# Weight parts kept by the second token group, retention chunks cut at the token blocks, and five early product pairs in an FFN

## The chip, the cores and the metric

The kernel runs on one core of one Trainium2 chip. TensorE (PE) multiplies matrices into PSUM, which has 8 banks; VectorE (DVE), ScalarE (ACT) and GpSimd (POOL) work beside it; SyncE (SP) issues most of the DMAs. The metric is the device time of one execution in microseconds. The time before is 2477.27 us, the median of 3 runs (2476.28 to 2477.57).

## What is computed

One layer of a hybrid decoder for 2048 prompt tokens and 8 sample tokens (one new token for each of 8 sequences), all in float32. Cut to what matters:

```python
h = rmsnorm(x, g_mix) * (1 + scale_m) + shift_m
q, k, v, g_ret, x_lru, g_lru = split(h @ w_in)          # 1024 -> 4*512 + 2*512
o, s_ret = retention(rotary(q), rotary(k), v, s_ret)     # 4 heads of 128, chunkwise
ret_out = silu(g_ret) * groupnorm(o)
hl = rg_lru(causal_dwconv(x_lru))                        # 512 channels, a scan over time
lru_out = hl * gelu(g_lru)
x = x + gate_m * (concat(ret_out, lru_out) @ w_out)
h = rmsnorm(x, g_ffn) * (1 + scale_f) + shift_f
f = (gelu(causal_dwconv(h @ w_up_conv)) * (h @ w_up_gate)) @ w_down   # 1024 -> 2816 -> 1024
x = x + gate_f * f
y = rmsnorm(x, g_final)
```

The six shifts, scales and gates come from the conditioning vector c by one more matrix, w_ada. The retention, LRU and convolution states are outputs too. Retention may be cut into chunks of any width: a chunk's scores are taken within it, and the state carries the rest.

## The kernel before

**Precision.** Each float32 operand is split into a high part that TensorE's reduced float32 holds and a low part, the rest; each product is three matmuls (`mm3`, L356: high by high, high by low, low by high, lines 358 to 360). Splitting a 128x512 piece of a weight (`parts`, L283) is a copy on ACT (L288) and a subtraction (L289) on the engine `lo_on`, POOL or DVE. The two parts, 128x1024, are written to a DRAM tile named by their key (L295), and whoever fetches the key later loads both parts from there (L286) and splits nothing. A w_in tile of 128 columns has two halves, each a key with `(h,)` added; w_out and w_down keys are one 128x512 piece; FFN keys are one left operand of a product (below). The first eight parts written in the first group are parked in `unsaved` and stored between items 4 and 7 (L1382).

**Groups and blocks.** The tokens go through the layer in three groups (`GROUPS`, L38): 688, 680 and 680 prompt tokens, the third with the 8 sample tokens behind them. A group has two blocks of 344 (340 in the second). Activations lie with channels on the partitions, so a matmul streams one block, 344 columns.

**Items.** `group_items` (L1180) writes each group's work as a list of items: weight keys, a rate, and a function. The main loop (L1379) fetches keys ahead of the items (`LOOK` is 4, a w_in or w_ada key counts 2), runs the function, and then advances two lists of generators: `soon` (normalisations, LRU chains) by the rate's whole part, and `bg` (the retention of a head) by the rate as a credit, 1 where it is 2. The order in one group: head 0, LRU 0, head 1, out-projection of head 0 (16 items), LRU 1, head 2, out of head 1 (16 items at rate 0.5), LRU 2 and 3, head 3 (its items by block: Q, K, V, gate of block 0, then of block 1), out of heads 2 and 3 (16 items of 12 matmuls, block 0 first), then the FFN. An out item of heads 2 and 3 waits until the retention of head 3 has ended its block.

The list sets priorities and the order of dependences; the framework's planner then fixes each engine's own order when the kernel is built, by its model of durations. Each engine runs its list in order. A tile comes from a pool with a fixed number of buffers, and whoever asks for one more waits for a release: the pool `f` has 12 (FFN operands and mixer outputs), `t` 10 (block-sized scratch), PSUM `pm` 3 (projections, down products, some early FFN products) and `pt` 5.

**Retention** (`ret`, L617) runs through chunks of 128 tokens with a shorter last one (six in a group). Step i does part a of chunk i (transposes, scores), part b of chunk i-1 (output and state) and part c of chunk i-2 (normalised and gated output). When the last chunk that touches a block is through part c, the block is split for the out-projection (L686). In the third group the sample tokens' steps (`ret_samples`, L692) are run at step `at`: 0, or 3 for head 3. The rate of head 3's block-1 items is 0.5 (L1196).

**FFN.** The 22 tiles of 128 channels are taken in 11 pairs, and each pair, for each of the two up-projections, with the two blocks and the two halves of the 1024 inputs, is a 2x2 block product with seven products in place of eight (`PRODUCTS`, L51): P1 and P2 need only block 0 (b11, b21); P5 needs t1, P6 t2, P3 b22, P7 t3 and P4 t4, which are made on DVE and ACT from both blocks (`operands2`, L925). P1 is added into several results: for an ordinary pair by going on in its PSUM bank, for an `apart` pair by DVE from a copy (`keep`, L997). In each group four pairs of products P1 and P2 come early, those of pairs 0 and 1 of both kinds, before the operands of block 1 are there; pair 1 is `apart`, with P1 and P2 in two banks of `pm`. P2's result goes through `up_out` (copy, convolution, GeLU) or `gate_out` (multiply, split into f tiles). Behind pair i come the 16 down items of pair i-1, between its products.

In the first group the 14 left operands of pair 0 are prepared ahead (`ahead`, L1272): split, stored and dropped, one behind each item of rate 0.5 or more from the out-projection of head 1 on.

Of the kernel before, what the change touches and what calls it, by code (L numbers as in the profile page):

```python
# [57 lines left out]
WIDTHS = sorted({w for _, n, _, _ in GROUPS for w in ((P,) if n % P == 0 else (P, n % P))}, reverse=True)  # L58
# [32 lines left out]
def hybrid_step(ctx: ExitStack, tc: tile.TileContext, I, O):  # L91
# [169 lines left out]
    unsaved = []  # L261
# [20 lines left out]

    def parts(key, w, src=None, lo_on=G):  # L283

        if src is None:
            nc.sync.dma_start(out=w.bitcast(F32), in_=split[key])  # L286
        else:
            S.activation(out=w[:, 0:512], in_=src, func=AF.Copy)  # L288
            lo_on.tensor_tensor(out=w[:, 512:1024], in0=src, in1=w[:, 0:512].bitcast(F32), op=ALU.subtract)  # L289
            nm = "_".join(str(v) for v in key)  # L290
            split[key] = dp.tile([P, 1024], F32, tag=nm, name=nm)
            if len(unsaved) < 2 * FIRST:
                unsaved.append((split[key], w))
            else:
                nc.sync.dma_start(out=split[key], in_=w.bitcast(F32))  # L295
        return [w[:, 512 * i:512 * i + 512].rearrange("p (k c) -> p k c", c=P) for i in range(2)]
# [29 lines left out]
    def fetch_operand(key, lo_on):  # L326
# [25 lines left out]
        if i == 1 and nm in ("A11", "A12"):  # L352
# [106 lines left out]
    class Group:  # L459
        def __init__(g, gi):  # L460
# [4 lines left out]
            g.chunks = [(c, min(P, g.ntok - c)) for c in range(0, g.ntok, P)]  # L465
# [151 lines left out]
        def ret(g, p):  # L617
# [46 lines left out]
            at = 0 if p < H - 1 else LAG + 1  # L664
            for i in range(nch + LAG):
# [16 lines left out]
                if 0 <= i - LAG:  # L682
                    part_c(*g.chunks[i - LAG], pst("oT") if q is None else q[:, 384:512])
                    for b in g.blocks:
                        if i == nch + LAG - 1 if b[1] == g.TC else sum(g.chunks[i - LAG]) >= b[1] > g.chunks[i - LAG][0]:
# [311 lines left out]
        def keep(g, q, name, more=None):  # L997
            t = ttile(name)
# [7 lines left out]
        def quad_item(g, st, kind, i, what, out, apart):  # L1006

            left, right, bank, start = PRODUCTS[what]
            early = what in ("P1", "P2") and i < 2
            q = g.product(st, (kind, i, left), right, bank, start or apart and what == "P6",  # L1010
                          psm if early and (apart or what == "P2") else pst)
            p1 = st.get("p1")
            if what == "P1":
                st["p1"] = g.keep(q, "p1")
# [4 lines left out]
            elif what == "P2":  # L1019
                out(2 * i, 0, q, p1, apart)  # L1020
                if not apart:
                    del st["p1"]
# [7 lines left out]
        def up_out(g, ft, l, q, more, stays=False):  # L1030
# [49 lines left out]
        def gate_out(g, ft, l, q, more, stays=False):  # L1080
            n = g.n
            cv = g.cv.pop((ft, l))[:, 0:n]
            if more is not None:
                t = (ttile("gv") if stays else more)[:, 0:n]
# [95 lines left out]
    def group_items(g, nxt):  # L1180
# [6 lines left out]
        def head(p, by_block=False):  # L1187
# [5 lines left out]
            for n, (j, b) in enumerate(jb):  # L1193
                if n == 4 and early:
                    add([], 0, lambda: (drain(bg), bg.append(g.ret(p))))
                add([("w_in", 512 * j + P * p)] if b == g.blocks[0] else [], 0.5 if n >= 4 and early else 1,  # L1196
# [37 lines left out]
        def quad(kind, i, what, rate=1):  # L1234
            st = quads.setdefault((kind, i), {})
            out_fn = g.up_out if kind == "w_up_conv" else g.gate_out
            add([(kind, i, PRODUCTS[what][0])], rate, g.quad_item, st, kind, i, what, out_fn, i == 1)
# [18 lines left out]
        UP, GATE = "w_up_conv", "w_up_gate"  # L1256
        seq = ("P1", "P5", "P6", "P2", "P7", "P3", "P4")
# [3 lines left out]
        out.extend(out_((0,), both, 0.25))  # L1261
        lru(1)
        head(2)
        n = len(out)
# [25 lines left out]
        for i in range(1, np_):  # L1290
# [3 lines left out]
            some = [(kind, what) for kind in (UP, GATE) for what in seq if i > 1 or what not in ("P1", "P2")]  # L1294
# [84 lines left out]
    for n, (keys, rate, fn, a) in enumerate(items):  # L1379
        if FIRST <= n < 2 * FIRST:  # L1380
            for dst, w in unsaved[2 * (n - FIRST):2 * (n - FIRST) + 2]:
                nc.sync.dma_start(out=dst, in_=w.bitcast(F32))  # L1382
        if n == 3:
# [50 lines left out]
```

## Time and profile before

| | us |
|---|---|
| median of 3 runs | 2477.27 |
| the profiled execution | 2479.54 |
| its span, first to last instruction | 2477.8 |
| TensorE busy in it | 2376.3 |
| mean granted TensorE clock | 0.984 of full |

The span is what the profile covers; the execution's own time is 1.7 us longer. A granted clock under 1.00 in a stretch means that TensorE ran part of it at half speed. The stretches that matter in each group are these (us from the start of the span):

| | first group | second | third |
|---|---|---|---|
| first projection of head 0 | 29.8 | 899.1 | 1669.0 |
| out-projection of head 1 | 229.9 | 1059.1 | 1837.6 |
| head 3 | 320.5 | 1117.2 | 1899.3 |
| out-projection of heads 2 and 3 | 353.9 | 1148.8 | 1933.6 |
| first FFN product | 401.0 | 1191.5 | 1986.3 |
| last down product | 899.3 | 1669.1 | 2466.1 |

### The profile page before, as it was taken

How to read it: one execution, taken by the hardware profiler on the slowest of the kernel's cores; microseconds unless marked ns; L12 is line 12 of the kernel's file. 1: busy time of each engine (PE TensorE's matmuls, PEld its weight loads, DVE VectorE, ACT ScalarE, POOL GpSimd, SP SyncE). 2: the span in 40 equal slices, each digit the busy share in tenths (PEclk: the TensorE clock that was granted, in tenths of full speed). 3: DMA queues.
4: the chain of work that ended last, by engine and by line, in shares of the span. 5: the costliest groups of instructions: out<-in, count | busy, mean ns of one | idle time of the engine just before them, and what ended most of it. 6: DMA issues, size and time to landing. Idle time of an engine off the chain costs nothing.

```text
span 2477.8 us, 40044 instructions
## 1 busy us (share of the span) xinstructions
PE 2376.3 (96%) x15157; PEld 2279.8 (92%) x15157; DVE 1433.9 (58%) x3159; ACT 857.4 (35%) x1935; POOL 701.5 (28%) x729
## 2 busy tenths in 40 slices
PE   6999888999999999999899999999999889999998
PEld 4988688999999899999899999999998889999998
DVE  4645567866676665665753434346666575454444
ACT  4323453544444534232422222243125242222222
POOL 3443440466666723222001010112123100101011
PEclk8999889999999999999999999999999999999999
DMA  9576875788878865333666676765332455667674
GB/s 347 179 259 212 298 249 191 265 291 297 303 285 308 313 226 180 116 110 120 210 216 244 215 246 214 252 215 193 131 121 89 147 209 200 243 214 245 213 249 165
DMA packets 233220, 543.89 MB, mean 220 GB/s; under 512 B 19191, under 2 KB 100711, under 8 KB 233020
## 3 DMA queue, kind: packets, MB, share of 16 engines
q1 hardware_dynamic: 231948, 539.87, 62.6%
q8 instruction: 120, 1.97, 0.3%
q10 hardware_dynamic: 696, 0.91, 0.1%
q0 software_dynamic: 384, 0.56, 0.1%
q14 instruction: 72, 0.59, 0.1%
HBM read 392.96 MB, written 148.42 MB: 218 GB/s over the span
## 4 chain that ended last, share of the span: by engine, by line
PE 57%; DVE 5%; issue 1%; ACT 1%; DMA 1%; POOL 1%; POOLq 0%; SPq 0%; DVEq 0%; ACTq 0%
PE down L359 6%; PE down L358 6%; PE down L360 6%; PE qx L359 4%; PE qx L360 4%; PE qx L358 4%; PE proj L358 4%; PE proj L360 4%; PE proj L359 4%; PE qz L358 2%; PE qz L359 2%; PE qz L360 2%; PE qy L359 1%; PE qy L360 1%; PE qy L358 1%
## 5 line engine op out<-in xcount | busy, mean ns | idle before, releaser
L836 DVE SCALAR_TENSOR_TENSOR x<-down,mod,x 128x344 f32<-128x344 f32 (+2 forms) x624 | 348.2, 568 | 351.4 <-PE down L360 346.8
L358 PE MATMUL proj<-hh,wb 128*128 128x344 f32 (+1 forms) x1152 | 380.5, 330 | 10.5 <-DVE rotb L609 4.3
L359 PE MATMUL proj<-hl,wb 128*128 128x344 f32 (+1 forms) x1152 | 373.7, 324 | 0.0
L360 PE MATMUL proj<-hh,wb 128*128 128x344 f32 (+1 forms) x1152 | 373.7, 325 | 0.0
L359 PE MATMUL qx<-op,wb 128*128 128x344 f32 (+1 forms) x1056 | 337.6, 320 | 5.9 <-DVE op L906 5.8
L443 POOL TENSOR_TENSOR ffl<-cv,ffh 128x344 fp32r<-128x344 f32 (+1 forms) x120 | 123.6, 1036 | 764.0 <-ACT ffh L442 696.9
L358 PE MATMUL qx<-op,wb 128*128 128x344 f32 (+1 forms) x1056 | 336.9, 320 | 2.7 <-ACT op L905 1.4
L360 PE MATMUL qx<-op,wb 128*128 128x344 f32 (+1 forms) x1056 | 336.5, 319 | 0.0
L358 PE MATMUL down<-ffh,wb 128*128 128x344 f32 (+1 forms) x960 | 305.0, 324 | 5.1 <-DVE x L836 5.0
L360 PE MATMUL down<-ffh,wb 128*128 128x344 f32 (+1 forms) x960 | 306.2, 320 | 0.3 <-POOL wb L289 0.3
L359 PE MATMUL down<-ffl,wb 128*128 128x344 f32 (+1 forms) x960 | 306.1, 319 | 0.0
L289 POOL TENSOR_TENSOR wb<-wr,wb 128x512 fp32r<-128x512 f32 x146 | 203.5, 1402 | 167.3 <-ACT wb L288 138.3
L358 PEld LDWEIGHTS proj<-hh,wb 128*128 128x128 f32 x1152 | 219.3, 190 | 25.1 <-issue 11.2
L359 PEld LDWEIGHTS proj<-hl,wb 128*128 128x128 f32 x1152 | 219.9, 191 | 2.6 <-issue 0.6
L360 PEld LDWEIGHTS proj<-hh,wb 128*128 128x128 f32 x1152 | 219.3, 190 | 2.5 <-issue 0.9
L359 PEld LDWEIGHTS qx<-op,wb 128*128 128x128 f32 x1056 | 198.6, 188 | 7.6 <-DVE op L906 7.6
L358 PEld LDWEIGHTS qx<-op,wb 128*128 128x128 f32 x1056 | 198.6, 188 | 3.9 <-ACT op L905 2.0
L1061 DVE SCALAR_TENSOR_TENSOR cv<-u,vec,cv 128x344 f32<-128x344 f32 (+2 forms) x264 | 171.4, 667 | 48.5 <-ACT cv L1041 46.5
L360 PEld LDWEIGHTS qx<-op,wb 128*128 128x128 f32 x1056 | 198.4, 188 | 0.0
L358 PEld LDWEIGHTS down<-ffh,wb 128*128 128x128 f32 x960 | 179.3, 188 | 11.1 <-DVE x L836 10.2
L360 PEld LDWEIGHTS down<-ffh,wb 128*128 128x128 f32 x960 | 180.4, 188 | 0.8 <-POOL wb L289 0.8
L359 PEld LDWEIGHTS down<-ffl,wb 128*128 128x128 f32 x960 | 180.6, 188 | 0.0
(313 smaller groups left out, 4856.4 us busy)
## 6 DMA issues: line engine op xcount, KB each, us to landing
wb<-w_down SPq DMA_DIRECT2D x100, 512.0 KB
wb<-w_in SPq DMA_DIRECT2D x96, 512.0 KB
wb<-w_up_conv_S SPq DMA_DIRECT2D x92, 512.0 KB
wb<-w_up_gate_S SPq DMA_DIRECT2D x92, 512.0 KB
wb<-w_up_conv_A SPq DMA_DIRECT2D x69, 512.0 KB
wb<-w_up_gate_A SPq DMA_DIRECT2D x69, 512.0 KB
w_in<-wb SPq DMA_DIRECT2D x48, 512.0 KB
w_up_conv_S<-wb SPq DMA_DIRECT2D x44, 512.0 KB
```

What stands on the lines that cost most here:

```text
L289: lo_on.tensor_tensor(out=w[:, 512:1024], in0=src, in1=w[:, 0:512].bitcast(F32), op=ALU.subtract)
L358: T.matmul(out, wh, xh, start=first, stop=False, skip_group_check=more)
L359: T.matmul(out, wh, xl, start=False, stop=False, skip_group_check=more)
L360: T.matmul(out, wl, xh, start=False, stop=last, skip_group_check=more)
L443: G.tensor_tensor(out=lo[:, 0:n], in0=src, in1=hi[:, 0:n].bitcast(F32), op=ALU.subtract)
L836: V.scalar_tensor_tensor(out=xs, in0=q[:, 0:np_], scalar=modv[:, jg, m, 0:1], in1=xs, op0=ALU.mult, op1=ALU.add)
L1061: V.scalar_tensor_tensor(out=cv[:, 0:np_], in0=u[:, j:j + np_], scalar=cfw[:, j, ft:ft + 1], in1=cv[:, 0:np_], op0=ALU.mult, op1=ALU.add)
```

## The change

- **Weight parts.** `unsaved` is gone. For the keys that `late` names (w_in tiles of heads 0 and 3 and of LRU 2 and 3, so 24 of the 48 halves, and w_out rows of heads 2 and 3, 8 of 16 pieces) the first fetch splits and stores nothing; the second group fetches the raw piece again, splits it again and stores it; the third loads the parts.
- **Chunks** end with the blocks: 128, 128, 88 twice in the first group (128, 128, 84 in the second; 88 and 80 in the third), six as before. The samples' steps of head 3 run at step 5, and head 3's block-1 items have rate 1.
- **Early pairs.** Five: pairs 0 and 1 of both kinds and pair 2 of `w_up_conv`. The last three are `apart`, and their P1 and P2 now go into one bank of `pm`: P1 is copied, and P2 is added on top in PSUM. P1 of the three come first, then P2 of the three. Pair 1's P1 copies lie in f tiles.
- **Ahead.** The 14 operands of pair 0 are spread: 0.45 of one per full item, from LRU 1 on.
- The raw A11 and A12 of pair 2 of `w_up_conv` are loaded twice, the low parts of pair 2's weights are made on DVE in the first group, and the small transposes and LRU constants come at item 6 in place of 3.

```diff
+def chunks_of(gi):
+    _, n, _, edges = GROUPS[gi]
+    ends = [min(e, n) for e in edges]
+    return [(c, min(P, e - c)) for s, e in zip(ends, ends[1:]) for c in range(s, e, P)]
...
-    unsaved = []
+    once = set()
...
+    def late(key):
+        kind, a = key[0], key[1]
+        if kind == "w_in":
+            t = a // P
+            return t % 4 == 3 or t >= 16 and t % 4 == 2 or t < 16 and t % 4 == 0
+        return kind == "w_out" and a % 512 >= 2 * P
...
+            if late(key) and key not in once:
+                once.add(key)
+                return [w[:, 512 * i:512 * i + 512].rearrange("p (k c) -> p k c", c=P) for i in range(2)]
             split[key] = dp.tile([P, 1024], F32, tag=nm, name=nm)
-            if len(unsaved) < 2 * FIRST:
-                unsaved.append((split[key], w))
-            else:
-                nc.sync.dma_start(out=split[key], in_=w.bitcast(F32))
+            nc.sync.dma_start(out=split[key], in_=w.bitcast(F32))
...
-        if i == 1 and nm in ("A11", "A12"):
+        if (i == 1 or i == 2 and kind == "w_up_conv") and nm in ("A11", "A12"):
             del pr[nm]
...
-            at = 0 if p < H - 1 else LAG + 1
+            at = 0 if p < H - 1 else nch - 1
...
-                        if i == nch + LAG - 1 if b[1] == g.TC else sum(g.chunks[i - LAG]) >= b[1] > g.chunks[i - LAG][0]:
+                        if sum(g.chunks[i - LAG]) == b[0] + g.npr(b):
...
             left, right, bank, start = PRODUCTS[what]
-            early = what in ("P1", "P2") and i < 2
-            q = g.product(st, (kind, i, left), right, bank, start or apart and what == "P6",
-                          psm if early and (apart or what == "P2") else pst)
+            if apart:
+                bank = "y" if what in ("P1", "P2") else bank
+                start = what in ("P1", "P5", "P6")
+            q = g.product(st, (kind, i, left), right, bank, start,
+                          psm if bank == "y" and i < 3 else pst)
             p1 = st.get("p1")
             if what == "P1":
-                st["p1"] = g.keep(q, "p1")
+                st["p1"] = g.keep(q, "p1", pool=fp if i == 1 else None)
...
-                out(2 * i, 0, q, p1, apart)
-                if not apart:
-                    del st["p1"]
+                out(2 * i, 0, q, None if apart else st.pop("p1"))
...
-                add([("w_in", 512 * j + P * p)] if b == g.blocks[0] else [], 0.5 if n >= 4 and early else 1,
+                add([("w_in", 512 * j + P * p)] if b == g.blocks[0] else [], 1,
...
+        early = ((UP, 1), (GATE, 1), (UP, 2))
...
         out.extend(out_((0,), both, 0.25))
+        n = len(out)
         lru(1)
         head(2)
-        n = len(out)
...
+        due = 0.0
         for it in its:
             out.append(it)
-            if ahead and it[1] >= 0.5:
+            due += 0.45 * min(it[1], 1)
+            if ahead and due >= 1:
+                due -= 1
                 key = ahead.pop(0)
                 add([key], 0, units.pop, key)
-        for i in range(2):
-            for kind in (UP, GATE):
-                for what in ("P1", "P2"):
-                    quad(kind, i, what, 3)
+        for kind in (UP, GATE):
+            for what in ("P1", "P2"):
+                quad(kind, 0, what, 3)
+        for what in ("P1", "P2"):
+            for kind, i in early:
+                quad(kind, i, what, 3)
...
-        if n == 3:
+        if n == 6:
...
-            near = k[0] == "w_out" and k[1] % 512 >= 2 * P or k[0] in ("w_up_conv", "w_up_gate") and k[1] < 2
+            near = k[0] == "w_out" and k[1] % 512 >= 2 * P or k[0] in ("w_up_conv", "w_up_gate") and k[1] < 3
```

More of the change, by code (lines that the diff above doesn't have):

```diff
@@ L55 @@
 LEFT = {v[0] for v in PRODUCTS.values()}
-WIDTHS = sorted({w for _, n, _, _ in GROUPS for w in ((P,) if n % P == 0 else (P, n % P))}, reverse=True)
+def chunks_of(gi):
+    _, n, _, edges = GROUPS[gi]
+    ends = [min(e, n) for e in edges]
+    return [(c, min(P, e - c)) for s, e in zip(ends, ends[1:]) for c in range(s, e, P)]
+WIDTHS = sorted({w for gi in range(len(GROUPS)) for _, w in chunks_of(gi)}, reverse=True)
 C_ID, C_TRI, C_MS, C_EP, C_QM, C_SP, C_KD = 0, 128, 256, 260, 264, 280, 292
@@ L464, in __init__ @@
             g.blocks = list(zip(edges, edges[1:]))
-            g.chunks = [(c, min(P, g.ntok - c)) for c in range(0, g.ntok, P)]
+            g.chunks = chunks_of(gi)
             g.pieces = [(c, min(P, g.TC - c)) for c in range(0, g.TC, P)]
@@ L995, in product, with keep @@
             return q
-        def keep(g, q, name, more=None):
-            t = ttile(name)
+        def keep(g, q, name, more=None, pool=None):
+            t = ttile(name) if pool is None else pool.tile([P, BMAX], F32, tag="f", name=name)
             with tc.high_priority(offset=2 * HASTE):
@@ L1028, in quad_item, with up_out @@
                 out(2 * i + 1, 0, q, st.pop("p1") if apart else None)
-        def up_out(g, ft, l, q, more, stays=False):
+        def up_out(g, ft, l, q, more):
             n = g.n
@@ L1078, in fhome, with gate_out @@
             return [g.flast[:, 2 * (ft % 2) + i, b[0]:b[1]] for i in range(2)]
-        def gate_out(g, ft, l, q, more, stays=False):
+        def gate_out(g, ft, l, q, more):
             n = g.n
@@ L1083, in gate_out @@
             if more is not None:
-                t = (ttile("gv") if stays else more)[:, 0:n]
+                t = more[:, 0:n]
                 with tc.high_priority(offset=2 * HASTE):
@@ L1236, in quad @@
             out_fn = g.up_out if kind == "w_up_conv" else g.gate_out
-            add([(kind, i, PRODUCTS[what][0])], rate, g.quad_item, st, kind, i, what, out_fn, i == 1)
+            add([(kind, i, PRODUCTS[what][0])], rate, g.quad_item, st, kind, i, what, out_fn, (kind, i) in early)
         def dn(ii, order, rate=1):
@@ L1293, in group_items @@
             d = dn((i - 1,), both) if i < np_ - 1 else []
-            some = [(kind, what) for kind in (UP, GATE) for what in seq if i > 1 or what not in ("P1", "P2")]
+            some = [(kind, what) for kind in (UP, GATE) for what in seq
+                    if (kind, i) not in early or what not in ("P1", "P2")]
             for n, (kind, what) in enumerate(some):
@@ L1379, in hybrid_step @@
     for n, (keys, rate, fn, a) in enumerate(items):
-        if FIRST <= n < 2 * FIRST:
-            for dst, w in unsaved[2 * (n - FIRST):2 * (n - FIRST) + 2]:
-                nc.sync.dma_start(out=dst, in_=w.bitcast(F32))
-        if n == 3:
+        if n == 6:
             for i in range(1, len(stage)):
```

## The prediction

> **What bounds the kernel now.** First the page: the span, TensorE's share of it, and the slices.
>
> ```profile
> span 2477.8 us, 40044 instructions
> ...
> PE 2376.3 (96%) x15157; PEld 2279.8 (92%) x15157; DVE 1433.9 (58%) x3159; ACT 857.4 (35%) x1935; POOL 701.5 (28%) x729
> ...
> PE   6999888999999999999899999999999889999998
> ...
> PEclk8999889999999999999999999999999999999999
> ```
>
> TensorE bounds it: 101.5 us of the span are left idle. No other engine is near its limit on average, so only stretches in which PE waits, or runs at a lower granted clock, can be won. The slices put them at the start, in the first group before its FFN, and at each group's change to its FFN. The windows name them; each row is the stretch, its length, and the busy time of PE, PEld, DVE, ACT, POOL, then clock, DMA share, GB/s.
>
> ```profile
> core 0: us, PE busy (x) PEld busy (x) DVE busy (x) ACT busy (x) POOL busy (x), PEclk, DMA share, GB/s
> 40.00:63.00 23.00, 17.89 (x91) 16.90 (x90) 20.03 (x46) 15.94 (x43) 10.05 (x11) 0.73 1.07 372
> 172.00:229.00 57.00, 57.00 (x371) 49.84 (x370) 29.39 (x58) 22.69 (x38) 25.75 (x26) 1.00 0.61 199
> 229.00:283.00 54.00, 47.30 (x278) 36.07 (x277) 32.76 (x88) 15.88 (x32) 15.54 (x20) 0.87 0.95 333
> 283.00:353.50 70.50, 66.01 (x398) 59.22 (x399) 50.24 (x82) 47.62 (x89) 36.12 (x34) 0.95 0.79 266
> 353.50:376.00 22.50, 17.42 (x105) 15.77 (x104) 13.79 (x47) 3.52 (x10) 5.77 (x13) 0.85 0.35 126
> 400.00:473.00 73.00, 62.65 (x368) 59.12 (x367) 63.22 (x126) 35.44 (x86) 17.77 (x11) 0.95 0.69 240
> ...
> 500.00:850.00 350.00, 344.98 (x2166) 339.45 (x2164) 234.23 (x344) 163.23 (x374) 235.66 (x179) 1.00 0.82 295
> ...
> 1080.00:1148.00 68.00, 67.95 (x426) 65.11 (x426) 40.98 (x76) 29.10 (x47) 20.04 (x22) 1.00 0.39 126
> 1148.50:1163.00 14.50, 11.63 (x83) 10.43 (x82) 9.20 (x36) 2.26 (x8) 4.98 (x11) 1.00 0.15 53
> 1191.00:1231.00 40.00, 32.94 (x197) 30.92 (x196) 33.52 (x78) 17.20 (x44) 4.22 (x3) 0.96 0.64 224
> 1250.00:1600.00 350.00, 350.00 (x2250) 350.00 (x2249) 157.43 (x301) 87.44 (x224) 32.55 (x33) 1.00 0.66 230
> 1933.50:1958.00 24.50, 17.86 (x110) 14.22 (x109) 15.20 (x52) 3.55 (x11) 5.68 (x13) 0.79 0.21 72
> 1986.00:2030.00 44.00, 35.62 (x193) 33.45 (x192) 35.31 (x99) 18.90 (x46) 2.94 (x3) 0.88 0.56 203
> ```
>
> I count a stretch's loss as PE's idle time plus (1 - clock) times its busy time. Start (40): 5.1 + 4.8 = 9.9. First group, second out-projection (229): 6.7 + 6.2 = 12.8, with DMA at 333 GB/s; then 4.5 + 3.3 = 7.8; last head's retention (353.5) 5.1 + 2.6 = 7.7; change to the FFN (400) 10.4 + 3.1 = 13.5. Second group: retention 2.9, FFN change 7.1 + 1.3 = 8.4. Third: 6.6 + 3.8 = 10.4 and 8.4 + 4.3 = 12.7. That is 86 us, 57 idle and 29 clock, and the change touches all nine. The steady FFN has nothing to win: 350 of 350 busy, 2250 matmuls, so 0.156 us each.
>
> **The start.** The eight parked stores go (two halves for each of head 0's four weight tiles, which are all late ones now).
>
> ```profile
> 42.20 2.83 SPq L1382 DMA_DIRECT2D w_in<-wb  x4
> ...
> 47.65 0.52 SPq L532 DMA_DIRECT2D rope<-in_rope  x1
> ...
> 56.79 0.62 PE L358 MATMUL proj<-hh,wb 128*128 128x344 f32 x1 [4.14 <-DVE sp_y L227]
> ```
>
> Four of them sit on SP ahead of the rotary table, 2.83 us of issue, and 4 x 524 KB at 372 GB/s are 5.6 us of DMA. Item 2 waits 4.14 us, since two product banks wait for the rotary work and the third for the normalisation of block 1; the small transposes now at item 6 stood in front of that too. Gain between 0 (the normalisation is late anyway) and 9.9: I take 4 (2.5 idle, 1.5 clock), the nearest row being the 4.14.
>
> **First group, 229 to 353.5.** The weight parts of FFN pair 0, made ahead, stand one behind each item of the second out-projection.
>
> ```profile
> w_up_conv_S<-wb SPq DMA_DIRECT2D x4, 512.0 KB
> w_up_gate_S<-wb SPq DMA_DIRECT2D x4, 512.0 KB
> ...
> w_up_gate_A<-wb SPq DMA_DIRECT2D x3, 512.0 KB
> ...
> w_up_conv_A<-wb SPq DMA_DIRECT2D x2, 512.0 KB
> ```
>
> So 13 of 14 fall into 229 to 283. By the new count (0.45 for a full item, 0.225 for one of these) the 12 full items before give 5.4 and the 16 here 3.6; 9 leave, each 0.52 MB stored and about 0.15 MB loaded: 6 of the window's 18 MB (54 us x 333 GB/s). 12 MB in 54 us are 220 GB/s, below the 230 at which 1250 to 1600 runs without idle. The five go to 172 to 229 and add 59 GB/s to 199; with 57 of 57 us busy there, LOOK ahead covers it. Gain 0 to 12.8; I take 7 (4 + 3). In 283 to 353.5, 24 stores (12.6 MB) leave as well and five units come: 0 to 7.8, I take 2 (1.5 + 0.5), because DVE and ACT are at 50 and 48 of 70 there.
>
> **Retention of the last head.**
>
> ```profile
> 361.06 0.69 DVE L342 TENSOR_TENSOR ws<-wr 128x512 f32<-128x512 f32 x1 [2.57 <-DMA wr<-in_w_up_conv]
> ...
> 364.35 0.47 PE L659 MATMUL kvT<-cst,on 128*128 128x128 f32 x1 [5.08 <-DVE sT L632]
> ...
> 1943.27 0.76 PE L741 MATMUL os<-vts,sTs 8*128 8x128 f32 x2 [5.33 <-DVE sTs L729]
> ```
>
> Six chunks stay six, so the work is the same. But chunk 2 no longer reaches into block 1, and the rate of block 1's items goes from 0.5 to 1: four steps (0 to 3) run beside those items, where two did. Step 4, which ends block 0, is still on the path. In the third group the sample tokens' steps, which hold PE 5.33 us, move behind block 0's end, under its 8 out items of 12 matmuls (1.9 us each). In the first, DVE stood 2.57 us for a weight's DMA in the middle of this chain; with the DMA load gone that is earlier. Gains: 6 of 7.7 (4.5 + 1.5), 1.5 of 2.9, 7.5 of 10.4 (5 + 2.5); the low ends 2, 0 and 3, for step 4's own chain.
>
> **Change to the FFN.** A fifth pair with operands of block 0 alone adds P1 and P2: 24 matmuls x 0.156 = 3.75 us of cover per group.
>
> ```profile
> 1206.97 0.49 PE L360 MATMUL qz<-op,wb 128*128 128x340 f32 x1
> ...
> 1223.28 0.42 PE L359 MATMUL qx<-op,wb 128*128 128x340 f32 x1 [1.54 <-DVE op L906]
> ...
> L1061 DVE SCALAR_TENSOR_TENSOR cv<-u,vec,cv 128x340 f32<-128x340 f32 x4 | 2.2, 562 | 0.0
> ```
>
> DVE makes block 1's operands (33.5 of 40 us busy) and sets when t2 is whole, at 1223.28. If DVE is no slower, PE's idle time before that shrinks by the 3.75. DVE gains the fifth pair's two convolution steps (2 x 0.56) and loses two additions, as P1 and P2 of an apart pair now add in one bank: nothing net. ACT gets about five copies more, with 17 of 40 us busy: covered, and if not, each is on the operands' path at about half a us. P2's wait for P1's copy lies under the other pairs' P1. I take 4.5 in the second group (3.7 + 0.8) and 5.5 in the third (3.7 + 1.8). In the first, the fifth pair's two fresh parts are split on DVE, 2 x 0.78 (next fence): 3 (2.2 + 0.8). Ends: 0 and 13.5, 8.4, 12.7. Pair 2's other 12 splits leave POOL for DVE (12 x 0.78 = 9.4 us), and two raw tiles are loaded twice: from 500 to 850 DVE is idle 116 of 350 us and PE waits 5, so nothing; without that cover it would be the 9.4.
>
> **Second group.** 24 halves of w_in and 8 of w_out are split and stored again.
>
> ```profile
> L289 POOL TENSOR_TENSOR wb<-wr,wb 128x512 fp32r<-128x512 f32 x146 | 203.5, 1402 | 167.3 <-ACT wb L288 138.3 <-DMA wr<-in_w_in 9.0 <-DMA wr<-in_w_up_conv 6.0
> ...
> L289 DVE TENSOR_TENSOR wb<-wr,wb 128x512 fp32r<-128x512 f32 x28 | 21.4, 778 | 18.2 <-ACT wb L288 18.0
> ...
> L288 ACT ACTIVATE wb<-wr 128x512 fp32r<-128x512 f32 x174 | 107.2, 626 | 121.0 <-DMA wr<-in_w_in 36.4 <-DMA wr<-in_w_out 18.3 <-PE qy L360 15.8
> ...
> SPq L295 <- POOL wb L289: 311.7, 175, 11.4
> ...
> 310.88 3.04 POOL L289 TENSOR_TENSOR wb<-wr,wb 128x512 fp32r<-128x512 f32 x2
> ...
> 310.71 3.58 DVE L792 SCALAR_TENSOR_TENSOR xc<-xl,vec,xc 128x344 f32<-128x344 f32 x3
> ...
> L792 DVE SCALAR_TENSOR_TENSOR xc<-xl,vec,xc 128x336 f32<-128x336 f32 x12 | 6.8, 568 | 0.9 <-ACT xc L771 0.9
> ```
>
> POOL gets 24 x 1.40 = 33.7 us, ACT 32 x 0.63 = 20, DVE 8 x 0.78 = 6. From 1080 to 1148 POOL is busy 20 of 68, so it fits. But each store waits on SP for its split (175 such waits), with the next loads queued behind it, and DVE pays: three additions of L792 beside a split took 3.58 us, 1.19 each against 0.57. The nearest row with that work is the first group's own: 283 to 376 loses 15.5 us where the second group's stretch loses 0.05 + 2.9. So 0 to 15.5, and for the 8 halves at its start a third more: 0 to 20.7. I take 4. The Trainium skill (SBUF — State Buffer, Who interferes with whom) says that a DVE instruction with two SBUF inputs contends with a GpSimd instruction that reads SBUF; the 3.58 us agree, and by it all 33.7 us of POOL could slow DVE, still within the bound.
>
> **Sum.** 4 + 7 + 2 + 6 + 1.5 + 7.5 + 3 + 4.5 + 5.5 = 41 gained (28.6 idle, 12.4 clock), 4 lost: 37. The profiled execution took 2479.5 us, its span 2477.8; the sum gives 2442.5 for it. The median is 2477.3, 2.2 lower: **2440**.
>
> **Rivals.**
> - *DVE takes the cover.* The early copies delay block 1's operands by as much as PE gains: the three FFN terms (13) go, 2453. For: DVE 33.5 of 40 busy. Against: its own work hardly grows.
> - *The front of the first group stays.* Its DMA is spread, but rotary, LRU and splits on DVE, ACT and POOL hold it: 4 + 7 + 2 go, 2453. For: 50 of 70 us busy on DVE. Against: DMA 0.95 just where it idles.
> - *The second group pays all:* 16.7 more, 2457.
> - *The clock comes back whole.* If the short gaps that are left no longer lower it, 28.6 + 29.3 - 4 = 54 are won: 2423. Against: half clock (0.49 us for a matmul) at 1206.97, after a gap of under 2 us. The Trainium skill (TensorE: Matmul & The Clock Gate, Why this matters for your kernels) warns only of idle gaps over about 3 us; by that rule nearly every low stretch would go, but the row at 1206.97 speaks against it.
> - *Slower: pair 1's f tiles.* P1 of pair 1 now lies in two of the 12 f tiles until P4. Pair 0's FFN operands take 8 and the early gate 2 more: 12 of 12. If a thirteenth is asked for before pair 0's first four come back, P7, P3 and P4 of the gate each wait for up to 4 down items and a product (4 x 0.93 + 1.9 = 5.6 us): 3 x 5.6 x 3 groups = 50, so 2490. It decides as soon as the order asks one product too early; by the item list the four come back one item before.
> - *Not what it says.* The order is fixed when the kernel is built, by its planner; if out items and products land as now, 2477.
>
> **How the numbers follow.** Forecast 0.54; DVE 0.10; front 0.10; second group 0.09; clock 0.10; f tiles 0.05; nothing 0.02. Alone, the forecast spans 2425 to 2455. The range, 2416 to 2466, goes below the clock's case by 7 and above to two of the three dearer cases at once (2440 + 13 + 13). About 0.2% (5 us) is what a measurement tells from no change. Faster 0.91: all cases but the last two, less 0.02 for three dear cases together; same 0.04; slower 0.05.
>
> **What would show it.** No stores before 60 us, and item 2 without its 4 us wait; 229 to 283 near 220 GB/s with under 3 us idle; the first out item of the last heads without a 5 us gap in groups one and three; ten early products ahead of the first qz, idle to t2 about 2 us; the second group's last 110 us of attention under 4 us longer. It is wrong if new gaps stand in the second group's LRU items, if t2 is whole later than 32 us into the change to the FFN (1223.28 against 1191 now), or if pairs 0 to 2 show PE waits on f or bank releases.

## The result, and the profile after

The changed kernel takes 2463.14 us (median, 2458.59 to 2465.0); the kernel before took 2476.78 us beside it (2474.58 to 2477.57). The ratio is 0.9944, 95% interval 0.9926 to 0.9961: 13.6 us faster, where 37 were forecast. The direction holds and the time lies in the range; the size is little more than a third.

The profiled execution has a span of 2462.1 us, 15.7 less. First the page of the kernel after: the span, the busy times, the slices and the clock.

```profile
span 2462.1 us, 40114 instructions
...
PE 2359.8 (96%) x15157; PEld 2275.5 (92%) x15157; DVE 1452.9 (59%) x3181; ACT 869.6 (35%) x1964; POOL 716.9 (29%) x739
...
PE   5999998999999999999899999999999989999998
...
PEclk9999999999999999999999999999999999999999
```

TensorE's idle time is what it was: 2462.1 - 2359.8 = 102.3 us, before 101.5. The busy time of its 15157 matmuls fell by 16.5 us. Some 10 of these are clock: with a mean clock of 0.984 the old span lost 0.016 x 2477.8 = 39.6 us, with 0.988 the new one 29.5; the first digits 8 of the old clock line, now 9, show it. Where the other 6 us of busy time went is not shown here. The forecast had 12.4 us of clock and 28.6 of idle less 4, so the idle part of it did not come: idle time went in some places and came back in others. The windows of the kernel after (columns as in the prediction) show where:

```profile
core 0: us, PE busy (x) PEld busy (x) DVE busy (x) ACT busy (x) POOL busy (x), PEclk, DMA share, GB/s
40.00:63.00 23.00, 16.98 (x101) 15.64 (x101) 21.52 (x50) 16.90 (x44) 10.31 (x11) 0.85 0.76 232
171.00:234.00 63.00, 59.44 (x395) 52.36 (x391) 37.36 (x72) 23.93 (x43) 25.18 (x24) 1.00 0.62 204
234.50:263.00 28.50, 27.59 (x189) 21.35 (x190) 20.48 (x58) 6.63 (x15) 14.60 (x19) 1.00 0.89 306
263.00:346.50 83.50, 77.12 (x478) 68.72 (x477) 63.23 (x106) 53.79 (x102) 41.98 (x41) 0.98 0.59 185
346.50:386.00 39.50, 37.83 (x242) 36.78 (x239) 28.16 (x74) 15.38 (x33) 7.60 (x12) 0.96 0.42 148
386.00:460.00 74.00, 62.45 (x362) 59.34 (x360) 60.62 (x121) 38.07 (x92) 14.16 (x10) 0.93 0.70 246
...
1095.00:1117.00 22.00, 19.08 (x107) 17.50 (x106) 16.77 (x23) 15.13 (x26) 12.03 (x11) 0.92 0.39 132
1117.00:1188.00 71.00, 69.69 (x470) 68.82 (x469) 46.03 (x110) 23.36 (x48) 18.37 (x26) 1.00 0.37 135
1188.00:1232.00 44.00, 36.71 (x211) 34.72 (x210) 34.03 (x77) 19.00 (x51) 4.62 (x3) 0.92 0.64 223
1931.00:1974.00 43.00, 40.74 (x266) 37.95 (x264) 31.35 (x96) 11.39 (x27) 6.59 (x13) 0.96 0.40 141
1974.00:2017.00 43.00, 35.84 (x213) 34.25 (x214) 34.16 (x98) 21.51 (x54) 3.80 (x3) 0.96 0.62 216
```

With the prediction's measure (idle time plus the clock's share), the second out-projection (234.5) lost 12.8 us with what follows it and now 0.9; the first group's last out items (346.5) 7.7, now 3.2; the third's (1931) 10.4, now 3.9; 263 to 346.5 is as before (7.8, now 7.9). On the other side, 171 to 234 had no idle time and now has 3.6; 1095 to 1117, LRU 3 of the second group, is a new loss of 2.9 + 1.5; and the first two changes to the FFN lose 15.9 and 10.2 us where they lost 13.5 and 8.4, while the third loses 8.6 for 12.7.

The same by stages, each from its first matmul to the first of the next, out of the two traces:

| | forecast | before, us | after, us | gain |
|---|---|---|---|---|
| start and head 0, first group | 4 | 82.2 | 81.0 | 1.2 |
| first group, LRU 1 to LRU 3 | 9 | 147.6 | 139.2 | 8.4 |
| head 3 and its out items, groups 1, 2, 3 | 6, 1.5, 7.5 | 80.5, 74.3, 87.0 | 75.7, 71.0, 79.6 | 4.8, 3.3, 7.4 |
| first FFN product to last down product, groups 1, 2, 3 | 3, 4.5, 5.5 | 498.3, 477.6, 479.9 | 501.2, 480.0, 475.8 | -2.8, -2.4, 4.1 |
| second group, from the first group's end to LRU 3 | -4 | 217.9 | 229.8 | -12.0 |
| the rest (first group 0.5, third 3.7, the end -0.5) | 0 | | | 3.7 |
| sum | 37 | | | 15.7 |

Such a table is one execution against one. Kernels below whose first group has the same text differ in it by up to 4.4 us (848.6 to 853.0), so a verdict here rests on the medians of the runs, and the stages only say where.

### The profile page after: what moved, and what is told of

Same layout as the page of the kernel before. It is cut to its first block, busy times and chain, and to the rows that moved or that the text cites. A ratio compares the mean times of both kernels' runs of the same rounds, so it can differ in the third digit from the quotient of the medians.

```text
span 2462.1 us, 40114 instructions
## 1 busy us (share of the span) xinstructions
PE 2359.8 (96%) x15157; PEld 2275.5 (92%) x15157; DVE 1452.9 (59%) x3181; ACT 869.6 (35%) x1964; POOL 716.9 (29%) x739
## 4 chain that ended last, share of the span: by engine, by line
PE 53%; DVE 4%; ACT 2%; DMA 1%; issue 1%; POOL 1%; POOLq 0%; SPq 0%; ACTq 0%; DVEq 0%
PE down L374 6%; PE down L373 6%; PE down L375 6%; PE qx L374 4%; PE qx L375 4%; PE qx L373 4%; PE proj L373 3%; PE proj L375 3%; PE proj L374 3%; PE qz L373 2%; PE qz L374 2%; PE qz L375 2%; PE qy L374 1%; PE qy L373 1%; PE qy L375 1%
## 5 line engine op out<-in xcount | busy, mean ns | idle before, releaser
L374 PE MATMUL qx<-op,wb 128*128 128x344 f32 (+1 forms) x1020 | 325.5, 319 | 2.6 <-DVE op L921 2.6
L373 PE MATMUL qx<-op,wb 128*128 128x344 f32 (+1 forms) x1020 | 324.7, 320 | 1.2 <-ACT op L920 1.2
L375 PE MATMUL qx<-op,wb 128*128 128x344 f32 (+1 forms) x1020 | 324.5, 319 | 0.0
L304 POOL TENSOR_TENSOR wb<-wr,wb 128x512 fp32r<-128x512 f32 x164 | 223.9, 1376 | 230.7 <-ACT wb L303 222.1
L375 PEld LDWEIGHTS proj<-hh,wb 128*128 128x128 f32 x1152 | 218.7, 190 | 5.7 <-POOL wb L304 3.9
L374 PEld LDWEIGHTS qx<-op,wb 128*128 128x128 f32 x1020 | 191.7, 188 | 3.4 <-DVE op L921 3.4
L373 PEld LDWEIGHTS qx<-op,wb 128*128 128x128 f32 x1020 | 191.5, 188 | 2.0 <-ACT op L920 1.8
L375 PEld LDWEIGHTS qx<-op,wb 128*128 128x128 f32 x1020 | 191.4, 188 | 0.0
L373 PE MATMUL qz<-op,wb 128*128 128x344 f32 (+1 forms) x528 | 169.7, 325 | 14.6 <-ACT op L920 10.7
```

What stands on the lines that cost most here:

```text
L373: T.matmul(out, wh, xh, start=first, stop=False, skip_group_check=more)
L374: T.matmul(out, wh, xl, start=False, stop=False, skip_group_check=more)
L375: T.matmul(out, wl, xh, start=False, stop=last, skip_group_check=more)
```

## The experiments

Every experiment was run beside the kernel before, and each ratio is to that. Such an interval reaches some 4 us to either side, so two kernels whose medians differ by 3 us are not told apart. The diffs show the lines that matter; `...` stands for others between them.

**Undo the weight parts.** All keys split and stored in the first group, the first eight parked, as before; the rest as changed.

```diff
-            if late(key) and key not in once:
-                once.add(key)
-                return [w[:, 512 * i:512 * i + 512].rearrange("p (k c) -> p k c", c=P) for i in range(2)]
```

> The changed kernel (2463.1 us) with the weight parts as before: all kept by the first group, the first eight stores parked. Stage theory (read from the two traces: the second group's attention became 14 us longer, the start barely shorter): the second group gets its time back, the first loses a few us to stores; 2452 to 2460. The prediction's terms (second group pays 4, the start gains 4, 283 to 353.5 gains 2): 2465.

2445.13 us, ratio 0.9871 (0.9853 to 0.9889): 18.0 us faster than the whole change. Both expectations are missed, the forecast's by 20 us. The late parts are the dearest piece of the change. By stages most of the 18 lie in three places: from the first group's end to LRU 3 of the second (219.2 us against 229.8), in the first group's LRU 1 to LRU 3 (134.3 against 139.2) and in its FFN (497.0 against 501.2).

**Undo the chunks**, and with them the rates and the samples' step of head 3 (further lines, not shown).

```diff
-    return [(c, min(P, e - c)) for s, e in zip(ends, ends[1:]) for c in range(s, e, P)]
+    return [(c, min(P, n - c)) for c in range(0, n, P)]
```

> The changed kernel with chunks of 128 across the blocks, the samples' steps at step 3 and head 3's block-1 items at rate 0.5, as before. Stage theory: the three retention stretches come back, 7.7 - 2.9, 5.7 - 2.4 and 10.2 - 2.3 us, so 16 us more: 2479. The prediction's terms (6 + 1.5 + 7.5): 2478. A rival, that the waits only moved to other places: within 3 us of 2463.

2481.87 us, 1.0019 (1.0007 to 1.0031): the chunks with their rates and step are worth 18.7 us in the changed kernel, 3 to 4 more than either theory had. TensorE's waits in the third group, 1950 to 2010 of this kernel (what waited, for whom: us in total, times, longest), have the old one back:

```profile
PE os L756 <- DVE sTs L744: 5.3, 1, 5.3
```

In the kernel after, the longest in its stretch, 1931 to 1974, are these; the samples' steps are not among them:

```profile
PE down L373 <- ACT mix L457: 0.9, 1, 0.9
PE down L374 <- POOL mix L458: 0.7, 1, 0.7
PE down L373 <- DVE fs L858: 0.3, 1, 0.3
```

**Undo the spreading** of the parts made ahead.

```diff
-            due += 0.45 * min(it[1], 1)
-            if ahead and due >= 1:
-                due -= 1
+            if ahead and it[1] >= 0.5:
```

> The changed kernel with pair 0's operands prepared one behind each item of the out-projection of head 1, as before. Stage theory: that out-projection gets its 13 us back and head 2 gives up its 8: 2468. The prediction's terms (7 + 2, nothing lost in head 2): 2472.

2461.76 us, 0.9935 (0.992 to 0.9951): no difference, and both expectations are missed. Yet the stages moved: the out-projection of head 1 takes 44.7 us without the spreading and 28.4 with it, head 2 35.1 and 43.2. From LRU 1 to LRU 3 the spreading is 12.4 us ahead (151.6 against 139.2), and then it loses most of it in head 3, its out items and the FFN (the first group as a whole: 857.9 against 856.4).

**Undo the fifth early pair** and what came with it: four pairs, P1 and P2 of the apart ones in two banks, the early products in their old order, pair 2's splits on POOL and its raw tiles loaded once. The first of these lines is:

```diff
-        early = ((UP, 1), (GATE, 1), (UP, 2))
+        early = ((UP, 1), (GATE, 1))
```

> The changed kernel with four early pairs, P1 and P2 of pair 1 in two banks, pair 2's splits on POOL, as before. Stage theory (the FFN from first product to last down item became 2.9 and 2.4 us longer in groups one and two and 4.0 shorter in three): 2460 to 2464, no difference. The prediction's terms (3 + 4.5 + 5.5): 2476.

2456.78 us, 0.9912 (0.9896 to 0.9929): 6.4 us faster than with five, where the prediction made it 13 slower. The fifth pair, the shared bank and pair 2's splits were not undone one by one, so what follows on the fifth pair holds for the three together.

**Both undone**, weight parts and early pairs.

> u_late with the four early pairs of before as well, so retention chunks and the spread preparation alone. If the early pairs' cost of 6 us is theirs alone: 2437 to 2441. If it came from the first group's weights arriving late beside them, which u_late mended already (its first FFN change is 3.4 us shorter): 2443 to 2447.

2445.49 us, 0.9872 (0.9856 to 0.9888). This is what was expected if the cost of five pairs came from weights that arrive late beside them. With the old weight parts, four or five pairs are one (2445.5 and 2445.1); with the late ones five are 6.4 us dearer. The late parts cost 11.3 us with four pairs and 18.0 with five.

**The apart pairs first**, on the kernel with the old weight parts, so that P2 of pair 0, of both kinds, no longer holds two of the three `pm` banks ahead of them.

```diff
-        for kind in (UP, GATE):
-            for what in ("P1", "P2"):
-                quad(kind, 0, what, 3)
         for what in ("P1", "P2"):
             for kind, i in early:
                 quad(kind, i, what, 3)
+        for kind in (UP, GATE):
+            for what in ("P1", "P2"):
+                quad(kind, 0, what, 3)
```

> u_late (2445.1) with the order of the early products turned round: P1 then P2 of the three apart pairs first, pair 0's two behind them. Theory 'banks' (the fifth pair's cover is not used, since pair 0's P2 hold two of the three pm banks until DVE has added P1 to them, so that the built order has the same 60 early matmuls ahead of the first qz as before the change): the built order now has 84 ahead of it, and the wait before the first qz (1.7 us in group two) goes; 24 x 0.156 us in three groups, 2434 to 2440. Rival 'DVE' (block 1's operands set the end whatever PE does first): 2443 to 2447.

2453.1 us, 0.9899 (0.9881 to 0.9917): no gain, outside both expectations, and by the medians 8 us slower (the profiled execution, 2444.73, is its fastest). The planner did put more ahead: 84 early matmuls stand before the first qz of the second group, where the whole change has 60. TensorE's timeline there shows what takes the place (start, duration, work, and in brackets the idle time before it and what ended it). The first wait is shorter, two longer ones come behind it, both for ScalarE's copies:

```profile
1183.37 0.58 PE L373 MATMUL qz<-op,wb 128*128 128x340 f32 x2 [0.91 <-ACT op L920]
...
1195.40 0.65 PE L373 MATMUL qy<-op,wb 128*128 128x340 f32 x1 [3.35 <-ACT u L1053]
1201.93 0.65 PE L373 MATMUL qx<-op,wb 128*128 128x340 f32 x1 [3.02 <-ACT p L1016]
```

**Split again, store nothing**, on the kernel with the old weight parts, as the next two. The first group splits and stores all keys as before; the second splits the late ones again and does not store them.

```diff
+    def saved(key):
...
+        if late(key) and key not in once:
+            once.add(key)
+            return False
+        return True
...
-                          None if key in split else load_rows_of
+                          None if saved(key) else load_rows_of
```

> u_late, but the second group fetches the raw pieces of the late keys again and splits them again without storing them. If the second group's 9 us are the splits' work on POOL, ACT and DVE: head 0 and LRU 3 of group two take 39 and 22 us again, 2452 to 2455. If they are the stores behind them in SP's queue: 2444 to 2447.

2456.71 us, 0.9923 (0.9909 to 0.9938): 11.6 dearer than without. Head 0 of the second group takes 39.5 us and LRU 3 22.1 (35.3 and 17.5 where the parts are loaded; 39.4 and 21.9 in the whole change). From the first group's end to LRU 3 of the second it is 228.0 us against 219.2, so 8.8 of the 11.6 lie there; another 3.3 stand in the first group, whose text is the same in both. The splits cost some 9 to 12 us, without any store behind them. The only wait of TensorE from 1090 to 1113, around LRU 3, is this one, which the kernel that loads the parts does not have:

```profile
PE zr L828 <- DVE xc L819: 3.0, 1, 3.0
```

**Store again, split nothing.** The second group loads the late parts and writes them back.

```diff
             nc.sync.dma_start(out=w.bitcast(F32), in_=split[key])
+            if late(key) and key not in once:
+                once.add(key)
+                nc.sync.dma_start(out=split[key], in_=w.bitcast(F32))
```

> u_late, but the second group, which loads the late keys' parts, stores them once more from the loaded tile, with no split. The stores' theory: 2452 to 2455. The splits' theory: 2444 to 2447.

2448.17 us, 0.9882 (0.9865 to 0.9899): 3 us dearer, between the two expectations; the ranges of the runs overlap, and the stretch to LRU 3 takes 218.7 us, no longer than without the stores. So such stores are not the price. (They wait for a load; stores that wait for a split were not tried without the rest.)

**No second subtraction.** As *split again, store nothing*, with the low part loaded from the stored parts and only the high part copied from the raw piece.

```diff
             if key in split:
+                nc.sync.dma_start(out=w[:, 512:1024].bitcast(F32), in_=split[key][:, 512:1024])
+            else:
                 lo_on.tensor_tensor(out=w[:, 512:1024], in0=src, in1=w[:, 0:512].bitcast(F32), op=ALU.subtract)
```

> The kernel in which the second group splits the late weights again without storing them (2456.7), but with the low part of these loaded from the stored parts and only the high part copied by ScalarE from a raw piece: the 24 subtractions of GpSimd and 8 of VectorE are gone, the raw loads, the ScalarE copies and the longer chain stay, and each piece moves 256 KB more. Theory 'GpSimd's subtractions slow VectorE': head 0 of the second group falls from 39.5 to 34 to 36 us and LRU 3 from 22.1 to 17.5 to 19, total 2445 to 2449. Rival 'the raw pieces and ScalarE's copies are what comes late': head 0 stays at 38 to 40 and LRU 3 at 21 to 22, total 2454 to 2458.

2447.6 us, 0.9894 (0.9879 to 0.9909): 9.1 of the 11.6 us are gone with the subtractions, though the raw loads, ScalarE's copies and more DMA than before stay. By the stretch from the first group's end to LRU 3, 222.3 us, it is 5.7 of 8.8. LRU 3 falls to 17.5 us; head 0 only to 37.6, short of the 34 to 36 expected: what holds it there stays open, for with the stores alone it takes 37.3. The subtractions gone are 24 of GpSimd and 8 of VectorE; VectorE's belong to the out items behind head 3, and that stage, 70.9 us with them and without, shows nothing of them, so the price is GpSimd's. The rows of LRU 3 show the way. VectorE in the whole change:

```profile
1098.78 0.83 DVE L832 TENSOR_TENSOR_SCAN s<-xl,oc,ti 128x340 f32<-128x340 f32 x1
...
1102.94 0.34 DVE L831 TENSOR_SCALAR xl<-xl 128x340 f32<-128x340 f32 x1 [2.73 <-POOL s L827]
...
1104.08 1.57 DVE L832 TENSOR_TENSOR_SCAN s<-xl,oc,ti 128x340 f32<-128x340 f32 x1
...
1109.49 2.66 DVE L807 SCALAR_TENSOR_TENSOR xc<-xl,vec,xc 128x340 f32<-128x340 f32 x3
```

GpSimd beside it in the same kernel:

```profile
1100.74 1.29 POOL L304 TENSOR_TENSOR wb<-wr,wb 128x512 fp32r<-128x512 f32 x1 [2.80 <-ACT wb L303]
1101.98 0.92 POOL L827 TENSOR_TENSOR s<-s,xl 128x340 f32<-128x340 f32 x1
...
1104.89 1.83 POOL L304 TENSOR_TENSOR wb<-wr,wb 128x512 fp32r<-128x512 f32 x1
...
1109.68 1.50 POOL L304 TENSOR_TENSOR wb<-wr,wb 128x512 fp32r<-128x512 f32 x1
```

The split waits 2.80 us for its copy; GpSimd runs in order, so the LRU's own product `s` stands behind it, and VectorE waits 2.73 us for that product. Then the scan takes 1.57 us where that of the other block took 0.83, and three additions take 0.89 us each, with two more splits beside them. TensorE waits 2.9 us for the sum `xc` behind these, and the chain of work that ended last runs through just these steps: ScalarE's copy, the split, the product `s`, the scan, the additions. Without the subtractions the step that had waited (L846 there), the additions (L822) and the product (L842) have these rows, first VectorE:

```profile
1089.01 1.06 DVE L846 TENSOR_SCALAR xl<-xl 128x340 f32<-128x340 f32 x1
...
1094.42 1.77 DVE L822 SCALAR_TENSOR_TENSOR xc<-xl,vec,xc 128x340 f32<-128x340 f32 x3
```

and GpSimd:

```profile
1087.41 1.31 POOL L842 TENSOR_TENSOR s<-s,xl 128x340 f32<-128x340 f32 x1 [3.39 <-DVE xl L839]
```

Now GpSimd waits for VectorE and not the other way round, and the three additions take 0.59 each. Not all is mended: L846 takes 1.06 us for 0.34, and the scan behind it still 1.39, beside the LRU's own work on GpSimd.

**The chunks alone**, with their rates, the samples' step and the small loads at item 6. Weight parts, early pairs and the parts made ahead as before the change.

> Only the chunks and their rates of the change (and the small loads at item 6); weight parts, early pairs and the parts made ahead as before. Theory 'additive': the chunks are worth the 18.7 us that undoing them cost, 2456 to 2460, and the spreading the rest down to 2445, some 11 to 13. Rival 'the spreading is worth nothing with the old weight parts either, as with the changed ones': 2444 to 2448, so that the chunks are worth about 31 us here.

2451.58 us, 0.9909 (0.9892 to 0.9925), between the two expectations: 23.2 us faster than before (2474.74 in this comparison), and the spreading on top of it (2445.49) 6.1.

**The spreading, without head 2.** Chunks as changed, all else as before, the parts made ahead spread at the same 0.45 but counted from the out-projection of head 1 on.

```diff
-        n = len(out)
         lru(1)
         head(2)
+        n = len(out)
         out.extend(out_((1,), both, 0.5))
```

> The chunks as changed, all else as before the change (weight parts, early pairs), and the FFN parts made ahead spread at the same 0.45 per full item, but counted from the out-projection of head 1 on, so that no unit falls into LRU 1 and head 2. Theory 'units in head 2 hold SP': head 2 of the first group falls from 42 to 35 us as in the kernel without spreading, the out-projection of head 1 keeps most of its 13 us (28 to 33), and the time is 2438 to 2442 (the kernel without this shift took 2445.5). Rival 'the DMA volume of the first group is the limit, the units only move': what head 2 wins the out-projection of head 1, the LRU or the last out items give back, 2444 to 2448.

2440.74 us, 0.9863 (0.9846 to 0.9879), within the first theory's range and the fastest version: 34.0 us under the kernel before, 22.4 under the change as made, 4.8 under the one that spreads from LRU 1 on (their runs overlap a little: up to 2445.39 here, from 2443.89 there). Head 2 takes 35.1 us, the out-projection 29.4. Part of head 2's 43.2 in the change is work that moved there (22 matmuls of the retention, 265 against 243), but 3.6 us are idle. SP's waits from 171 to 234 in the whole change begin with these:

```profile
SPq L310 <- POOL wb L304: 13.4, 4, 4.9
SPq L281 <- DVE ws L357: 11.1, 1, 11.1
```

The load of a raw piece of w_ada (L281) stood 11.1 us for a raw tile that VectorE's sums for the parts made ahead still held, and SP issues in order, so the w_in pieces of head 2 stood behind it. Without units in head 2 (191 to 227) SP's list is two lines long and that wait is gone:

```profile
SPq L310 <- POOL wb L304: 18.1, 6, 6.4
SPq L281 <- PE ada L397: 9.4, 3, 6.3
```

**Three early pairs** in that fastest version: P1 and P2 of pair 1 of w_up_gate go back.

```diff
-        early = ((UP, 1), (GATE, 1))
+        early = ((UP, 1),)
```

> The fastest kernel so far (chunks as changed, parts made ahead spread from the out-projection of head 1 on, weight parts as before, four early pairs: 2440.7) with one early pair fewer: P1 and P2 of pair 1 of w_up_gate go back to their place behind the operands of block 1. The prediction's arithmetic run backwards: 24 matmuls of 0.156 us less to run while those operands are made, 3.75 us a group, 11.2 in all, 2450 to 2454. Theory 'no cover': what an early pair adds is taken back by VectorE's and ScalarE's copies ahead of the operands and by the few banks, so the time until t2 is whole and the idle time do not change: 2437 to 2445, with t2 whole in the second group within 1 us of the four-pair kernel's, or earlier.

2451.15 us, 0.9894 (0.9877 to 0.9911): 10.4 us dearer, as the forecast's arithmetic has it (11.2). The theory 'no cover' falls as a general statement: the fourth pair is worth some 3.5 us a group, and the fifth, as it was made here, nothing. Sixty microseconds from the first FFN product of the second group, with three pairs, then with four, then with five in the whole change:

```profile
1171.60:1231.60 60.00, 51.78 (x295) 49.17 (x295) 41.48 (x94) 22.83 (x60) 6.05 (x5) 0.89 0.60 210
```

```profile
1165.50:1225.50 60.00, 53.10 (x324) 50.84 (x323) 42.97 (x96) 24.32 (x64) 6.99 (x6) 0.97 0.68 230
```

```profile
1188.10:1248.10 60.00, 52.71 (x313) 50.72 (x313) 40.26 (x90) 24.15 (x63) 7.34 (x6) 0.94 0.67 228
```

From three to four pairs 29 more matmuls are done; 1.3 us of that is idle time, the rest the clock, 0.89 to 0.97. With the fifth, 11 fewer are done; with five pairs and the old weight parts it is 311 at 0.94, so the late parts are not the reason.

## Why the prediction was wrong in size

**Two terms of the sum failed: the cover of the early pairs (13 us, measured nothing or a loss) and the second group's splits (4 us, measured 9 to 12).** With 0 and 12 in their places, 37 becomes 37 - 13 - 8 = 16, and the profiled execution won 15.7. That the two agree so well is luck: the start gave 2.8 us less than its term, and stages without a term gave 3.7.

*The early pairs.* The prediction held that a fifth pair adds 3.75 us of cover, if VectorE is no slower. The windows up to the first qz of the second group answer it; before:

```profile
1191.50:1205.60 14.10, 11.77 (x80) 11.28 (x79) 8.39 (x25) 1.92 (x4) 0.85 (x1) 1.00 0.88 318
```

and after:

```profile
1188.10:1202.20 14.10, 11.78 (x80) 11.29 (x79) 8.39 (x25) 1.91 (x4) 0.85 (x1) 1.00 0.85 311
```

The same 80 matmuls in the same 14.10 us: the fifth pair puts nothing ahead of the first wait. The prediction looked for ten early products ahead of the first qz; of their 120 matmuls 60 stand there, and of the 96 before the change it was 60 too. This alone is not the reason: with three pairs it is 60 as well, and the fourth, all of it behind the first wait, was worth 10.4 us. The matmuls behind it lie among those of P5 and P6. They cover the waits for t2, but the fifth pair's bring waits for ScalarE's copies that were not there at this length:

```profile
1202.20 0.58 PE L373 MATMUL qz<-op,wb 128*128 128x340 f32 x2 [1.73 <-ACT op L920]
...
1213.31 0.42 PE L374 MATMUL qx<-op,wb 128*128 128x340 f32 x1 [0.80 <-DVE op L921]
1216.39 0.42 PE L373 MATMUL qy<-op,wb 128*128 128x340 f32 x1 [1.73 <-ACT p L1016]
1226.87 0.42 PE L373 MATMUL qz<-op,wb 128*128 128x340 f32 x1 [2.08 <-ACT p L1016]
```

The first wait has stayed. In the 60 us from the first product of the second group, TensorE waits 4.4 us for P6's operands (L921) with three pairs, 2.4 with four and 0.8 with five; for copies of banks (L1016) 0, 0.6 and 3.8. So what the fifth pair covers it loses to copies. The wait of 1.54 us for t2 is down to 0.80, much as forecast, but 1.73 us came as P2 of an apart pair, which waits for P1 to be copied out of the bank that the two now share, and 2.08 us as a wait for P5's copy. So "P2's wait for P1's copy lies under the other pairs' P1" did not hold, and a wait for a bank's release was one of the prediction's own signs of being wrong. The third group's FFN did gain 4.1 us, but not by the fifth pair: with the chunks alone, and four pairs, it takes 476.3 us, with the whole change 475.8. The rival *DVE takes the cover* had the outcome (three terms gone) with chance 0.10; the engine was ScalarE and its copies of banks. The error in the step: "ACT about five copies more, covered" was read from its share of 17 of 40 us, while TensorE's waits name single copies. That it is their place in ScalarE's order, and why the planned order gives no earlier one, is shown only so far: with the apart pairs first, the waits moved behind the first one and the time was no better.

*The second group's splits.* The bounds, 0 to 20.7, hold the measured 11.6; the value 4 was too near the low end. The prediction priced the additions beside a split and SP's queue. The stores cost some 3 us, which the runs cannot tell from none (store again), and the subtractions are 9.1 of 11.6 (no second subtraction). What the sum lacked is that GpSimd's list also carries a step of the LRU chain, which then stands behind a split that waits for ScalarE. "From 1080 to 1148 POOL is busy 20 of 68, so it fits" was the wrong test: GpSimd had room, the chain through it had none. New gaps in the second group's LRU items were the sign that the prediction had named for this.

*The weight parts as a whole* were to win 2 us (4 at the start, 2 from 283 to 353.5, less 4) and cost 18.0. Beyond the second group, the term of 2 for the stores that leave the first group came out as a loss. LRU 3 of the first group takes 27.9 us with the late parts and 23.5 in the kernel with the old ones, with the same wait for `xc` (2.5 us), which that kernel lacks. Why the splits crowd there when nothing is stored was not tried.

*What held.* The retention of head 3: 15 forecast, 15.5 by the stages, 18.7 and 23.2 by the two comparisons of runs, which hold the chunks, the rates and the samples' step together. What the latter have more lies in part outside head 3: with the chunks alone the second group takes 3.3 us less from its head 0 to LRU 3, and no term of the sum stood for that. The first group's out-projection: 9 forecast, 8.4 by the stages, but not as foreseen. The out-projection's stretch gained 13.4, and "LOOK ahead covers it" failed for the units moved to head 2: they kept raw tiles that SP's next load needed. Later stages of the first group gave back what was left, so that undoing the spreading alone changed nothing.

*The start.* 4 us forecast, 1.2 by the stages. The stores are gone from SP, and the wait is still there; it is the normalisation that is late, as the lower bound had it:

```profile
56.42 0.63 PE L373 MATMUL proj<-hh,wb 128*128 128x344 f32 x1 [4.23 <-DVE h L580]
```

*The other rivals.* That the front of the first group stays came true for the start alone (1.2 of 4); behind it 8.4 of 9 came. That the clock comes back whole has fallen: 0.988 after, and 0.92 from 1188 to 1232, where no gap is over 2.1 us. The f tiles show no sign of running out: TensorE has no such row of waits of some 5 us in the changes to the FFN, and the 50 us did not come. The second group paid 12.0 of the 20.7 by the stages.

*Open.* The late parts cost 6.7 us more with five early pairs than with four, and the second splitting makes up 11.6 of their 18.0. In the first group of the whole change, VectorE's sums for pair 1 stand still for a raw piece at the change to the FFN:

```profile
404.16 0.69 DVE L357 TENSOR_TENSOR ws<-ws,wr 128x512 f32<-128x512 f32 x1 [5.42 <-DMA wr<-in_w_up_conv]
```

and TensorE then waits 6.25 us at 406.60. The kernel with the late parts, five pairs and the old chunks has that stall too (5.58 us), those with either part undone have at most 2.42, save 3.70 with three pairs; but the one without the spreading does not have it and is no faster. So this stall is a part of the 6.7 us at most, and it was not tried alone.

## What to carry to other kernels

An engine with idle time may still be unable to take more work if its list carries a step of a chain: look for the step behind which the new work would stand, and for what waits on it, before the engine's share. Cover is only worth something ahead of the wait that it is to cover; count the matmuls that the order really puts there, and the waits that the added work brings itself. When one piece of a change wins and another loses, undo them one by one: here the chunks alone won 23 us of which the rest of the change gave 10 back.

## What the runs showed of the hardware

- The granted clock fell without any long gap. With three early pairs the second group's 60 us window had 8.2 us of idle time and ran at 0.89, and TensorE's waits in it (waiter, releaser, total, times, longest) are at most 2.3 us long:

```profile
PE qx L374 <- DVE op L921: 4.4, 3, 2.3
PE qz L373 <- ACT op L920: 1.7, 1, 1.7
PE qx L373 <- ACT op L920: 1.2, 1, 1.2
```

  From 1198.1 to 1208.3 it ran at 0.50; two gaps of 1.2 us stand just before and the one of 2.3 at its start. With four pairs (6.9 us idle, none over 1.8) the window ran at 0.97. So 1.3 us more of idle time came with some 4 us of clock (0.08 of 52 busy). The Trainium skill (TensorE: Matmul & The Clock Gate, Why this matters for your kernels) warns of idle gaps of more than about 3 us; here the clock fell beside gaps of 1 to 2.3 us that follow each other within 20 us. That it is their nearness was not tried by itself.
- VectorE beside GpSimd: the addition of 0.57 to 0.59 us took 0.89 and the scan of 0.83 took 1.57 with GpSimd's work beside them. Without the weights' splits that scan still took 1.39, so the splits are the smaller part of its loss. The Trainium skill (SBUF — State Buffer, Who interferes with whom) has the shared port; the trace agrees and adds the sizes. The wait for GpSimd's place in its order, 2.73 us, was the larger part of the loss at that place.
